# Taking the tensor work off GpSimd, and forming the low part of a weight by an adding DMA

## The chip, the cores and the metric

The program runs on one core of one Trainium2 chip, as one launch. The metric is the device time of an execution in microseconds. The kernel before took 2098.97 us (median of two runs, 2098.39 and 2099.54); its profiled execution has a span of 2094.1 us.

## The reference

Two layers of a hybrid encoder work on 512 tokens of width 1024, in float32. What matters of it:

```python
proj = h @ w_in                                   # z 1024, x/B/C 2048, dt 32, u 1024 columns
xbc  = silu(depthwise_conv_centred(xbc))          # five taps along the tokens
y    = ssd_chunked_scan(forward) + flipped(backward) + D * x      # 16 heads x 64, 4 groups, state 128
y_ssd = rms_norm(y * silu(z))
y5   = D u + Re(C s) of 64 complex diagonal recurrences, both directions   # the "S5" part
g    = gelu(y5);  y_s5 = rms_norm(g * sigmoid(g @ w_glu + b_glu))
h    = layer_norm(alpha * h + concat([y_ssd, y_s5]) @ w_out)
h    = layer_norm(alpha * h + square(relu(h @ w1)) @ w2)          # w1 1024x4096, w2 4096x1024
```

Nearly all matrix work is a product of activations with weights that are read once each: per layer 8 + 16 + 8 column tiles of w_in, 16 row blocks of w_out, 8 tiles of w_glu, 32 of w1 and 32 of w2, each 128 x 1024 floats (512 KB). Over both layers these are 240 "units".

## The kernel before, in words

**Three passes.** A product in float32 is made of three TensorE passes in the shortened type fp32r: with every operand split as high + low, `mm3` (L108 to L111) issues high x high, high x low and low x high. Each weight is split when it arrives. `load_raw` (L91) lets SP's queue bring the unit from DRAM into one of 2 buffers `raw`; `split` (L96) lets ScalarE copy it, rounded, into `whi` (L98), and then VectorE or GpSimd subtract, `wlo = raw - whi` (L99). `whi` and `wlo` have 3 buffers each. Which engine subtracts is written in a table `KN` (entries wu, wx, wz, glu); of the 224 wide units VectorE makes 166 and GpSimd 58. Sixteen units of a layer pair (the "wide" ones of `rows_proj`) are split in two halves of 512 columns.

**Stages.** Input layer norm; mixer of layer 0; its w_out in two parts (`rows_proj`, L678: the SSD half, then GLU, then the S5 half); the MLP of layer 0 (L889 up, `rows_proj` down, four quarters in turn); then the same for layer 1. In `rows_proj` four PSUM tiles rp0 to rp3 (one for each 128 tokens) take up units in pairs.

**The mixer** has two streams that a table `mrg` merges. The SSD stream (`ssd_group`, L566) works by pairs of heads: conv taps on VectorE from PSUM (L546 to L550; the last in some tiles by ScalarE and GpSimd, L554), two scans that make the decay mask E (L620, L621), the sum of two weighted copies `w + w2` (L628, GpSimd), `E * w` (L630), two products `eb` (L631, L632, GpSimd), `xd` (L592, GpSimd). The S5 stream makes input tables per batch (`s5_vtab`, L372: L385 to L387), runs a recurrence over 62 chunks (`s5_scan`, L409: four VectorE instructions of 64 elements for each of two parts at each step, L419 to L424, 992 in all), and makes output tables (`s5_wtab`, L426: L461 to L463). The tables are complex products of 512 elements, half on VectorE and half on GpSimd. Layer 0 makes its tables inside its mixer; those of layer 1 are made by a generator in between the units of layer 0's MLP, go to DRAM, and are loaded in layer 1's mixer.

**Other work of GpSimd:** squares of the MLP's hidden tiles (L904, 64 times), sums of squares for the RMS norms (L663, L665), parts of the first layer norm (L152 to L160), and powers of -0.5 for the norms (L150, L673).

**What sets the order.** Every engine runs its own instructions in one order, which a list scheduler at build time decides from priorities and a modelled time; `split` has high priority. Semaphores join the engines: a matmul of a unit waits for the split, the split for the landing of raw and for the last matmul of the unit three before.

Of the kernel before, what the change touches and what calls it, by code (L numbers as in the profile page):

```python
# [10 lines left out]
F32 = mybir.dt.float32  # L11
F32R = mybir.dt.float32r
I32 = mybir.dt.int32
AF = mybir.ActivationFunctionType
# [35 lines left out]
    wu=["GGGGGGGG", "VGGVGGGG"], wx=["GGGGGGGGGGGGGGGG", "GGGGGGGGGVGVGVGV"], wz=["GVGGGGGG", "GGGVGGGG"],  # L50
    em=["VVVVGVVG", "GGVGVVGV"], yz=["VVVVVVVG", "VVGGGVGG"], ct=["VVVVGGVVVVGVVVVV", "VVVVVVVVVGVVVVVG"], v0="VV",
    v1="GG", w0="VG", w1="GV", gv0="VG", gv1="GG", gw0="GV", gw1="VG", vb=(4, 2), gvb=(4, 3), cbb=2, wyb=4, raw=2,
    whi=3, wlo=3, nb=dict(mm=3, ss=1, sm=2, s5=2), po=[{}, {"scan": -150, "w": -35}], glu="VVVVGVVV", ln0="SVSG",
    sn=[2, 2], gen="110211101100201101103101",
# [4 lines left out]
def kernel(ctx: ExitStack, tc: tile.TileContext, A, out, depth=L):  # L59
# [80 lines left out]
    def layer_norm(pool, h, t, gb, hT, e=None):  # L140
# [10 lines left out]
        if e is G:  # L151
            G.tensor_scalar(x, x, mv[:, 0:1], rs, op0=ALU.subtract, op1=ALU.mult)  # L152
            G.tensor_tensor(x, x, gb[:, 0], op=ALU.mult)
            G.tensor_tensor(x, x, gb[:, 1], op=ALU.add)
        elif e is S:
            nb = pool.tile([128, 1], F32, tag="nb", name="nb", bufs=2)
            V.scalar_tensor_tensor(nb, mv[:, 0:1], -1.0, rs, op0=ALU.mult, op1=ALU.mult)
            S.activation(x, x, AF.Identity, scale=rs, bias=nb)
            V.tensor_tensor(x, x, gb[:, 0], op=ALU.mult)
            G.tensor_tensor(x, x, gb[:, 1], op=ALU.add)  # L160
        else:
            V.scalar_tensor_tensor(x, x, mv[:, 0:1], gb[:, 0], op0=ALU.subtract, op1=ALU.mult)
            V.scalar_tensor_tensor(x, x, rs, gb[:, 1], op0=ALU.mult, op1=ALU.add)
# [874 lines left out]
```

## Time and profile before

| | |
|---|---|
| median of the runs | 2098.97 us |
| span of the profiled execution | 2094.1 us |
| PE busy | 1754.4 us (84%) |
| DVE busy | 1418.6 us (68%) |
| POOL busy | 837.1 us (40%) |
| ACT busy | 725.5 us (35%) |
| DMA engines, mean share | q1 41.8% + q10 3.6% of 16 engines' span, 279.94 MB |

PE is TensorE, DVE VectorE, ACT ScalarE, POOL GpSimd, SP the engine that issues most loads. The busy time of an engine is a sum over stages that are bound by different things, so the rows below cut the span into stages: the start, mixer 0 and its first w_out half (0 to 633 us), GLU and second half (to 728), MLP 0 with the table generator (to 1197), mixer 1 and first half (to 1637), the rest of layer 1 (to 2065), the last norms.

### The profile page before, as it was taken

Reading aid. Unit: us, or ns where it says so; the run is one execution under the profiler, and the core shown is the slowest. Engines: PE = TensorE matmul, PEld = TensorE weight load, DVE = VectorE, ACT = ScalarE, POOL = GpSimd, SP = SyncE. Lnnn points to the kernel's source line nnn. Section 1 sums busy time; section 2 is a strip of 40 time slices with the busy share of each in tenths; the row PEclk is TensorE's granted clock in tenths of the full one; section 3 lists DMA queues with packets and bytes.
Section 4 is the critical chain, followed back from the end, with each engine's and each line's share of the span. In section 5 each row is a group of like instructions: output and inputs, shape, how many; then the busy total and the mean of one; then the engine's idle time right before and its main releaser. Section 6 shows DMA issues by size and latency. Waiting matters only on the chain.

```text
span 2094.1 us, 28322 instructions
## 1 busy us (share of the span) xinstructions
PE 1754.4 (84%) x10872; PEld 1427.8 (68%) x10872; DVE 1418.6 (68%) x2449; ACT 725.5 (35%) x1156; POOL 837.1 (40%) x557
## 2 busy tenths in 40 slices
PE   3677766676799995967899998776799999999998
PEld 3556555564578883745688887655677888888886
DVE  7468999999956767598733636999963564333335
ACT  2224433354215331211223336244563434232231
POOL 4456755445431128688702234344341112021121
PEclk8779887887799997979899999897999999999999
DMA  4655533434353355656533477542587233323232
GB/s 172 174 149 139 138 96 93 121 83 125 87 177 103 99 123 171 197 161 190 172 102 92 139 225 215 138 119 86 143 215 246 92 110 91 100 91 101 83 108 81
DMA packets 131239, 279.94 MB, mean 134 GB/s; under 512 B 12320, under 2 KB 58400, under 8 KB 130464
## 3 DMA queue, kind: packets, MB, share of 16 engines
q1 hardware_dynamic: 114144, 252.05, 41.8%
q10 hardware_dynamic: 16960, 26.09, 3.6%
q8 instruction: 85, 1.39, 0.3%
q14 instruction: 50, 0.41, 0.1%
HBM read 241.26 MB, written 36.83 MB: 133 GB/s over the span
## 4 chain that ended last, share of the span: by engine, by line
PE 44%; DVE 34%; DMA 9%; POOL 6%; issue 4%; ACT 1%; SPq 1%; POOLq 0%; DVEq 0%; ACTq 0%
PE rp L110 7%; PE rp L111 7%; PE rp L109 7%; PE up_ps L110 4%; PE up_ps L109 4%; PE up_ps L111 4%; DVE sc L422 4%; DVE XV L424 4%; DVE sc L420 4%; DVE sc L419 3%; DMA cb<-in_cb 3%; DMA Bv<-in_bb 2%; DVE E L620 2%; DVE E L621 1%; PE y L519 1%
## 5 line engine op out<-in xcount | busy, mean ns | idle before, releaser
L98 ACT ACTIVATE whi<-raw 128x1024 fp32r<-128x1024 f32 x224 | 236.2, 1057 | 494.9 <-PE rp L111 117.0
L99 DVE TENSOR_TENSOR wlo<-raw,whi 128x1024 fp32r<-128x1024 f32 x166 | 226.3, 1365 | 246.1 <-ACT whi L98 245.6
L904 POOL TENSOR_TENSOR hr<-hr 128x512 f32<-128x512 f32 x64 | 103.2, 1614 | 375.7 <-ACT hr L903 375.7
L99 POOL TENSOR_TENSOR wlo<-raw,whi 128x1024 fp32r<-128x1024 f32 x58 | 142.5, 2459 | 194.1 <-ACT whi L98 187.5
L109 PE MATMUL up_ps<-hThi,whi 128*128 128x512 f32 (+1 forms) x560 | 209.3, 376 | 3.5 <-ACT hr L903 3.2
L110 PE MATMUL up_ps<-hTlo,whi 128*128 128x512 f32 (+1 forms) x560 | 209.5, 375 | 0.1
L111 PE MATMUL up_ps<-hThi,wlo 128*128 128x512 f32 (+1 forms) x560 | 209.2, 374 | 0.0
L110 PE MATMUL rp<-wlo,ahi 128*128 128x512 f32 x448 | 184.0, 411 | 21.3 <-DVE wlo L99 21.3
L109 PE MATMUL rp<-whi,ahi 128*128 128x512 f32 x448 | 174.1, 410 | 21.5 <-ACT whi L98 13.1
L111 PE MATMUL rp<-whi,alo 128*128 128x512 f32 x448 | 182.8, 408 | 0.0
L109 PE MATMUL xbc_ps<-hThi,whi 128*128 128x512 f32 x256 | 113.6, 444 | 41.1 <-ACT z L649 23.6
L109 PEld LDWEIGHTS up_ps<-hThi,whi 128*128 128x128 f32 x560 | 105.9, 190 | 23.9 <-ACT hr L903 4.3
L111 PEld LDWEIGHTS up_ps<-hThi,wlo 128*128 128x128 f32 x560 | 106.4, 190 | 19.1 <-issue 0.4
L110 PEld LDWEIGHTS rp<-wlo,ahi 128*128 128x128 f32 x448 | 88.5, 197 | 44.8 <-DVE wlo L99 23.6
L110 PEld LDWEIGHTS up_ps<-hTlo,whi 128*128 128x128 f32 x560 | 106.3, 190 | 18.6 <-DVE hTlo L175 0.3
L109 PEld LDWEIGHTS rp<-whi,ahi 128*128 128x128 f32 x448 | 87.5, 196 | 43.8 <-ACT whi L98 14.4
L111 PE MATMUL xbc_ps<-hThi,wlo 128*128 128x512 f32 x256 | 111.2, 434 | 1.7 <-POOL wlo L99 1.7
L110 PE MATMUL xbc_ps<-hTlo,whi 128*128 128x512 f32 x256 | 111.4, 435 | 0.0
L908 DVE TENSOR_TENSOR alo<-hr,ahi 128x512 fp32r<-128x512 f32 x64 | 53.6, 839 | 76.6 <-ACT ahi L907 76.3
L111 PEld LDWEIGHTS rp<-whi,alo 128*128 128x128 f32 x448 | 88.3, 197 | 22.2
L422 DVE TENSOR_TENSOR sc<-sc,XV 128x64 f32<-128x64 f32 x248 | 101.9, 429 | 1.9
L420 DVE TENSOR_TENSOR sc<-XV,l 128x64 f32<-128x64 f32 x248 | 101.9, 411 | 0.0
(287 smaller groups left out, 4414.0 us busy)
## 6 DMA issues: line engine op xcount, KB each, us to landing
raw<-in_w SPq DMA_DIRECT2D x128, 512.0 KB
raw<-in_wi SPq DMA_DIRECT2D x64, 512.0 KB
Pv<-pd SPq DMA_DIRECT2D x32, 512.0 KB
ab<-ad SPq DMA_DIRECT2D x32, 512.0 KB
eb<-ad SPq DMA_DIRECT2D x32, 512.0 KB
raw<-in_wo SPq DMA_DIRECT2D x32, 512.0 KB
Bv<-in_bb SPq DMA_DIRECT2D x16, 512.0 KB
U<-Ud SPq DMA_DIRECT2D x128, 64.0 KB
```

The lines of the kernel that those rows point to most:

```text
L98: S.activation(hi, raw, AF.Copy)
L99: e.tensor_tensor(lo, raw, hi.bitcast(F32), op=ALU.subtract)
L109: PE.matmul(o, lhsT=sh, rhs=mh, start=first, stop=False)
L110: PE.matmul(o, lhsT=sh, rhs=ml, start=False, stop=False)
L111: PE.matmul(o, lhsT=sl, rhs=mh, start=False, stop=last)
L419: V.tensor_tensor(t2[i], x[:, ::-1, hs[i]], l8[:, 1, :, hs[i]], op=ALU.mult)
L420: V.tensor_tensor(t1[i], x[:, :, hs[i]], l8[:, 0, :, hs[i]], op=ALU.mult)
L422: V.tensor_tensor(t1[i], t1[i], x1[:, :, hs[i]], op=ALU.add)
L424: V.tensor_tensor(x1[:, :, hs[i]], t1[i], t2[i], op=ALU.add)
L620: V.tensor_tensor_scan(E2, ab[:, 0], C("md"), NEG, op0=ALU.add, op1=ALU.max)
L904: G.tensor_tensor(r, r, r, op=ALU.mult)
L908: V.tensor_tensor(hl, r, hh.bitcast(F32), op=ALU.subtract)
```

## The change

- **Weight split.** `whi` as before. `wlo` is now filled by ScalarE with the negated rounded weight (a second copy with scale -1), and then a DMA on GpSimd's queue reads the unit a second time from DRAM and adds it into `wlo` (224 DMAs of 512 KB and 32 of 256 KB). VectorE and GpSimd have no part in a split any more.
- **GpSimd's tensor work** goes to VectorE: conv tap, `w + w2`, all `E * w`, `eb`, `xd` (now read from PSUM), gate product, sums of squares, first layer norm. The square of a hidden tile is made twice: ScalarE squares into `ahi`, VectorE computes max(o,0) * r from PSUM. GpSimd keeps the -0.5 powers, a few memsets and the adding DMAs.
- **S5 tables**: for each batch and direction three VectorE products of 1024 elements in place of six of 512 on two engines. For this the sign is carried by a third slot (B, cp), and the powers lie in a replicated table `pw2`.
- **Recurrence**: one part of 128 elements in place of two of 64 (`sn` from 2 to 1): 496 instructions.
- **eb** is loaded as two pieces of 384 columns, 128 KB less for each head; buffers `vb` (4,2) to (3,2), `gvb` (4,3) to (3,2).

```diff
-    def split(hi, lo, raw, e):
+    def split(hi, lo, raw, src):
         with tc.high_priority():
             S.activation(hi, raw, AF.Copy)
-            e.tensor_tensor(lo, raw, hi.bitcast(F32), op=ALU.subtract)
+            S.activation(lo, raw, AF.Copy, scale=-1.0)
+            G.dma_start(lo, src, accum_op=ALU.add)
...
-            for ri, e in enumerate((e0, e1)[dd]):
-                t1 = pool.tile([128, 512], F32, tag="tv%d" % (e is G), name="tv", bufs=1)
-                e.tensor_tensor(v4(W[:, ri]), P[:, :, 0], v4(B[:, ri]), op=ALU.mult)
-                e.tensor_tensor(v4(t1), P[:, :, 1], v4(B[:, 1 - ri]), op=ALU.mult)
-                e.tensor_tensor(W[:, ri], W[:, ri], t1, op=ALU.add if ri else ALU.subtract)
+            t1 = pool.tile([128, 2, 512], F32, tag="tv", name="tv", bufs=1)
+            pb = lambda r: P[:, :, r].unsqueeze(1).to_broadcast([128, 2, 4, 128])
+            V.tensor_tensor(v4(W), pb(0), v4(B[:, 1:3]), op=ALU.mult)
+            V.tensor_tensor(v4(t1), pb(1), v4(B[:, 0:2]), op=ALU.mult)
+            V.tensor_tensor(W, W, t1, op=ALU.add)
...
-                G.tensor_tensor(xd, X[:, c0:c0 + 3].rearrange("p c (h q) -> p c h q", h=2),
+                V.tensor_tensor(xd, Xp[:, c0:c0 + 3].rearrange("p c (h q) -> p c h q", h=2),
...
-                G.tensor_tensor(w, w, w2, op=ALU.add)
+                V.tensor_tensor(w, w, w2, op=ALU.add)
                 Ev = E.rearrange("p (c n) -> p c n", c=4)
-                EN[KN["em"][l][ct]].tensor_tensor(Ev, Ev, w, op=ALU.mult)
-                G.tensor_tensor(eb[:, 0, 128:512], CT[:, 128:512], eb[:, 0, 128:512], op=ALU.mult)
-                G.tensor_tensor(eb[:, 1, 0:384], CT[:, 0:384], eb[:, 1, 0:384], op=ALU.mult)
+                V.tensor_tensor(Ev, Ev, w, op=ALU.mult)
+                V.tensor_tensor(eb[:, 0], CT[:, 128:512], eb[:, 0], op=ALU.mult)
+                V.tensor_tensor(eb[:, 1], CT[:, 0:384], eb[:, 1], op=ALU.mult)
...
                     S.activation(r, o, AF.Relu)
-                    G.tensor_tensor(r, r, r, op=ALU.mult)
                     hh = pool.tile([128, T], F32R, tag="ahi", name="ahi", bufs=8)
                     hl = pool.tile([128, T], F32R, tag="alo", name="alo", bufs=8)
-                    S.activation(hh, r, AF.Copy)
+                    S.activation(hh, r, AF.Square)
+                    V.scalar_tensor_tensor(r, o, 0.0, r, op0=ALU.max, op1=ALU.mult)
                     V.tensor_tensor(hl, r, hh.bitcast(F32), op=ALU.subtract)
```

GpSimd in the first mixer, before: splits, tables and SSD products stand in one queue.

```order
L99 TENSOR_TENSOR wlo<-raw,whi 128x1024 [waits DMAHW3_49,PE_49,Activation_49]
L631 TENSOR_TENSOR eb<-xbc,eb 128x384 [waits DMAHW0_49]
L632 TENSOR_TENSOR eb<-xbc,eb 128x384
L386 TENSOR_TENSOR tv<-Pv,Bv 128x512 [waits Pool_49]
...
L628 TENSOR_TENSOR w<-w,w_1781 128x512 [waits DVE_49,Activation_49]
L99 TENSOR_TENSOR wlo<-raw,whi 128x1024 [waits DMAHW3_49,PE_49,Activation_49]
L387 TENSOR_TENSOR Wv<-Wv,tv 128x512 [waits Pool_49]
L99 TENSOR_TENSOR wlo<-raw,whi 128x1024 [waits DMAHW6_49,PE_49,Activation_49]
L592 TENSOR_TENSOR xd<-Xrow,fac 128x384 [waits Activation_49]
```

The same queue after the change, from the start to the end of layer 0's first MLP units.

```order
L145 TENSOR_TENSOR rs<-ve,mhalf 128x1 x2
L94 DMA wlo<-in_wi 128x1024 x2
L145 TENSOR_TENSOR rs<-ve,mhalf 128x1 x2
L94 DMA wlo<-in_wi 128x1024 x30
L94 DMA wlo<-in_wo 128x1024 x5
L668 TENSOR_TENSOR r_ssd<-r_ssd,mhalf 128x4
L94 DMA wlo<-in_wo 128x1024 x3
L94 DMA wlo<-in_wg 128x1024 x8
...
L94 DMA alo<-in_wo 128x512 x6
L94 DMA wlo<-in_w 128x1024 x3
L145 TENSOR_TENSOR rs<-ve,mhalf 128x1 x4
L94 DMA wlo<-in_w 128x1024 x56
```

Nothing is left there but DMAs and small powers, and a power stands behind the DMAs written before it. Next, TensorE at the end of a w2 pair in the last MLP, before (names with their buffer numbers):

```order
L110 MATMUL rp2_15887<-wlo_15952,ahi_15677 128x512
L111 MATMUL rp2_15887<-whi_15951,alo_15678 128x512
L109 MATMUL rp0_15885<-whi_15957,ahi_15715 128x512 [waits Activation_49]
L109 MATMUL rp1_15886<-whi_15957,ahi_15715 128x512
L109 MATMUL rp2_15887<-whi_15957,ahi_15715 128x512
L109 MATMUL rp3_15888<-whi_15951,ahi_15639 128x512
L110 MATMUL rp3_15888<-wlo_15952,ahi_15639 128x512
L111 MATMUL rp3_15888<-whi_15951,alo_15640 128x512
L110 MATMUL rp0_15885<-wlo_15958,ahi_15715 128x512 [waits DVE_49]
```

and the place that corresponds to it after:

```order
L104 MATMUL rp0_15182<-whi_15257,ahi_15006 128x512 [waits Activation_49]
L104 MATMUL rp1_15183<-whi_15257,ahi_15006 128x512
L104 MATMUL rp2_15184<-whi_15257,ahi_15006 128x512
L105 MATMUL rp3_15185<-wlo_15251,ahi_14967 128x512
L106 MATMUL rp3_15185<-whi_15250,alo_14968 128x512
L104 MATMUL rp3_15185<-whi_15257,ahi_15006 128x512
L104 MATMUL up_ps_15325<-hThi_12735,whi_15320 128x512 [waits Activation_49]
L105 MATMUL up_ps_15325<-hTlo_12736,whi_15320 128x512
L105 MATMUL rp0_15182<-wlo_15258,ahi_15006 128x512 [waits DMASW3_49]
```

The first low-weight matmul of a unit waits for a DMA where it waited for VectorE, and more high-weight matmuls are drawn ahead of it; between the last use of the buffer's old content (wlo_15189) and this row stand 37 matmuls of 512 columns, 36 at the pair before. Last, ScalarE in such a pair after the change; before, there was one row for each unit, `whi`.

```order
L901 ACTIVATE ahi<-hr 128x512 [waits Activation_49]
L93 ACTIVATE wlo<-raw 128x1024 [waits DMAHW1_49,DMASW4_49,PE_49]
L92 ACTIVATE whi<-raw 128x1024 [waits PE_49]
L93 ACTIVATE wlo<-raw 128x1024 [waits DMAHW2_49,DMASW5_49,PE_49]
L92 ACTIVATE whi<-raw 128x1024 [waits PE_49,Activation_49]
```

The negated copy waits for raw, for the DMA that filled the buffer before, and for TensorE's last use of it; the next `whi` is queued behind it.

## Rows read from the trace of the kernel before

**Rows 1.** Windows by stage: busy us (and instructions) of each engine, clock, DMA.

```profile
core 0: us, PE busy (x) PEld busy (x) DVE busy (x) ACT busy (x) POOL busy (x), PEclk, DMA share, GB/s
0.00:633.00 633.00, 437.11 (x3387) 350.09 (x3388) 522.56 (x1010) 218.27 (x386) 330.86 (x223) 0.83 0.46 129
633.00:728.00 95.00, 95.00 (x424) 77.35 (x423) 62.49 (x76) 41.19 (x59) 17.99 (x13) 1.00 0.36 110
728.00:1197.00 469.00, 401.86 (x2193) 324.27 (x2192) 310.39 (x379) 119.02 (x169) 254.37 (x159) 0.92 0.49 147
1197.00:1637.00 440.00, 371.75 (x2840) 307.02 (x2839) 322.19 (x755) 203.12 (x358) 157.65 (x113) 0.92 0.59 171
1637.00:2065.00 428.00, 428.00 (x1947) 352.29 (x1946) 182.84 (x206) 143.89 (x188) 70.33 (x46) 1.00 0.32 97
```

**Rows 2.** Page, part 4: the chain that ended last, by engine.

```profile
PE 44%; DVE 34%; DMA 9%; POOL 6%; issue 4%; ACT 1%; SPq 1%; POOLq 0%; DVEq 0%; ACTq 0%
```

**Rows 3.** Timeline of DVE around 411 and 420 us: start, us, line.

```profile
411.33 0.25 DVE L419 TENSOR_TENSOR sc<-XV,l 128x64 f32<-128x64 f32 x1
...
417.78 1.22 DVE L621 TENSOR_TENSOR_SCAN E<-ab,E 128x512 f32<-128x512 f32 x1
...
419.87 1.00 DVE L420 TENSOR_TENSOR sc<-XV,l 128x64 f32<-128x64 f32 x1
...
421.77 2.42 DVE L420 TENSOR_TENSOR sc<-XV,l 128x64 f32<-128x64 f32 x1
```

**Rows 4.** Timeline of POOL, same stretch.

```profile
419.77 1.02 POOL L631 TENSOR_TENSOR eb<-xbc,eb 128x384 f32<-128x384 f32 x1
...
421.75 2.37 POOL L99 TENSOR_TENSOR wlo<-raw,whi 128x1024 fp32r<-128x1024 f32 x1
```

**Rows 5.** Windows of tile sc (recurrence), both mixers.

```profile
0.00:633.00 633.00, 200.76 (x496) 0.83 0.46 129
1197.00:1637.00 440.00, 162.31 (x496) 0.92 0.59 171
```

**Rows 6.** Windows of tile E on DVE (scans and products), both mixers.

```profile
0.00:633.00 633.00, 61.68 (x44) 0.83 0.46 129
1197.00:1637.00 440.00, 52.23 (x40) 0.92 0.59 171
```

**Rows 7.** Windows of tile wlo on DVE, both mixers.

```profile
0.00:633.00 633.00, 13.17 (x10) 0.83 0.46 129
...
1197.00:1637.00 440.00, 19.31 (x15) 0.92 0.59 171
```

**Rows 8.** Lines of DVE, 0 to 633 us: costliest and cheapest table line.

```profile
L461 DVE TENSOR_TENSOR Wy<-cp,pw 128x512 f32<-128x512 f32 x16 | 20.5, 1295 | 3.2 <-PE y L519 3.0
...
L463 DVE TENSOR_TENSOR Wy<-Wy,tw 128x512 f32<-128x512 f32 x16 | 15.4, 960 | 0.0
```

**Rows 9.** Lines by form, DVE, whole span: busy us, mean ns.

```profile
L645 DVE SCALAR_TENSOR_TENSOR xbc<-xbc,sp,y_ps 128x512 f32<-128x512 f32 x16 | 11.8, 740 | 6.8 <-PE y_ps L638 6.8
L99 DVE TENSOR_TENSOR alo<-raw,ahi 128x512 fp32r<-128x512 f32 x16 | 10.5, 688 | 12.0 <-ACT ahi L98 12.0
L253 DVE TENSOR_TENSOR pp_tb<-pw 128x128 f32<-128x128 f32 x4 | 1.1, 280 | 0.0
```

**Rows 10.** Tile wlo on DVE: duration in ns, min/median/max.

```profile
L99 DVE TENSOR_TENSOR wlo<-raw,whi x166: 1204/1225/2311, 182.2 to 2052.4; 128x1024 fp32r<-128x1024 f32 x166
```

**Rows 11.** Page, part 3: queue of the hardware DMAs.

```profile
q1 hardware_dynamic: 114144, 252.05, 41.8%
```

**Rows 12.** Windows: the slice of 50 us with the highest DMA share.

```profile
1550.00:1600.00 50.00, 47.96 (x465) 37.83 (x464) 17.22 (x28) 26.38 (x46) 16.03 (x15) 0.97 0.88 263
```

**Rows 13.** Timeline of SP's queue: a raw unit of 512 KB is issued.

```profile
1700.77 3.60 SPq L93 DMA_DIRECT2D raw<-in_w  x2
```

**Rows 14.** Timeline of ACT: the copy that waited for that unit.

```profile
1704.39 1.06 ACT L98 ACTIVATE whi<-raw 128x1024 fp32r<-128x1024 f32 x1 [1.84 <-DMA raw<-in_w]
```

**Rows 15.** Tile wlo on POOL: duration in ns, min/median/max.

```profile
L99 POOL TENSOR_TENSOR wlo<-raw,whi x58: 2335/2390/4258, 16.7 to 1650.1; 128x1024 fp32r<-128x1024 f32 x58
```

More of the change, by code (lines that the diff above doesn't have):

```diff
@@ L49 @@
           0, 0, 1, 1, 1, 0, 0, 0, 0, 5, 0, 0, 0, 2, 0, 0, 1, 0, 0, 0]],
[L50 to L54, printed above, removed]
+    vb=(3, 2), gvb=(3, 2), cbb=2, wyb=4, raw=2, whi=3, wlo=3, nb=dict(mm=3, ss=1, sm=2, s5=2),
+    po=[{}, {"scan": -150, "w": -35}], sn=[1, 1], gen="110211101100201101103101",
 )
@@ L128, in proj_tile, with proj_halves @@
         return o
-    def proj_halves(srcs, act, tag, name, es):
-        ws = [wunit(x, e) for x, e in zip(srcs, es)]
+    def proj_halves(srcs, act, tag, name):
+        ws = [wunit(x) for x in srcs]
         os_ = [psum(tag[i % len(tag)], name) for i in range(len(srcs))]
@@ L150, in layer_norm @@
         G.tensor_tensor(rs, ve, mhalf[:, 0:1], op=ALU.pow)
[L151 to L163, printed above, removed]
+        V.scalar_tensor_tensor(x, x, mv[:, 0:1], gb[:, 0], op0=ALU.subtract, op1=ALU.mult)
+        V.scalar_tensor_tensor(x, x, rs, gb[:, 1], op0=ALU.mult, op1=ALU.add)
         if hT is None:
@@ L256, in params @@
             V.tensor_tensor(o[:, 1], ta[:, 1, :, 0:m], tb_[:, 1, :, 0:m], op=ALU.add)
+        pw2 = per.tile([128, 2, 2, 8, 8, 8], F32, tag="pw2", name="pw2", bufs=1)
+        for ri in range(2):
+            for dd in range(2):
+                for x in range(2):
+                    S.activation(pw2[:, ri, dd, :, :, 4 * x:4 * x + 4],
+                                 pw[:, ri, dd, 1:9].rearrange("p k (m q) -> p k m q", q=4), AF.Copy)
         pd = dr.tile([2, 8, 32, 2, 128], F32, tag="pd", name="pd", bufs=2)
@@ L493, in s5_tables @@
         for m in range(8):
-            for dd, W in enumerate(s5_vtab(l, pool, prm, m, ens(KN["gv0"]), ens(KN["gv1"]), *KN["gvb"])):
+            for dd, W in enumerate(s5_vtab(l, pool, prm, m, *KN["gvb"])):
                 nc.scalar.dma_start(tb["V"][m, dd], W)
@@ L497, in s5_tables @@
         for m in range(8):
-            for dd, W in enumerate(s5_wtab(l, pool, prm, tb["KK"], m, "sm", ens(KN["gw0"]), ens(KN["gw1"]))):
+            for dd, W in enumerate(s5_wtab(l, pool, prm, tb["KK"], m, "sm")):
                 nc.scalar.dma_start(tb["W"][m, dd], W.rearrange("p r q i h -> p r (q i h)"))
@@ L615, in ssd_group @@
                 ab = pool.tile([128, 2, T], F32, tag="ab", name="ab", bufs=1)
-                eb = pool.tile([128, 2, T], F32, tag="eb", name="eb", bufs=2)
-                for i, x in enumerate((ab, eb)):
-                    nc.sync.dma_start(x,
-                                      dtp["ad"][:, hh, i].rearrange("d c s -> d (c s)").unsqueeze(0).to_broadcast([128, 2, T]))
+                eb = pool.tile([128, 2, 384], F32, tag="eb", name="eb", bufs=2)
+                nc.sync.dma_start(ab, dtp["ad"][:, hh, 0].rearrange("d c s -> d (c s)").unsqueeze(0).to_broadcast(
+                    [128, 2, T]))
+                for dd in range(2):
+                    nc.sync.dma_start(eb[:, dd], dtp["ad"][dd, hh, 1, 1 - dd:4 - dd].rearrange(
+                        "c s -> (c s)").unsqueeze(0).to_broadcast([128, 384]))
                 V.tensor_tensor_scan(E2, ab[:, 0], C("md"), NEG, op0=ALU.add, op1=ALU.max)
@@ L696, in rows_proj @@
                         lo = pool.tile([128, 512], F32R, tag=tl, name=tl, bufs=8)
-                        split(hi, lo, raw[:, i * 512:(i + 1) * 512], V)
+                        split(hi, lo, raw[:, i * 512:(i + 1) * 512], units[n, q][:, i * 512:(i + 1) * 512])
                         ws.append((hi, lo))
@@ L757 @@
         G.memset(XV[:, :, :, 0::127], 0.0)
-        os_ = proj_halves([A["wi"][l, 16 + m] for m in range(3)], act, ["mm"], "u_ps", ens(KN["wu"][l]))
+        os_ = proj_halves([A["wi"][l, 16 + m] for m in range(3)], act, ["mm"], "u_ps")
         with pool_("dt%d" % l) as pool:
@@ L769, in s5_stream @@
                     if i < 8:
-                        o = os_[i] if i < 3 else proj_tile(A["wi"][l, 16 + i], act, "mm", "u_ps", EN[KN["wu"][l][i]])
+                        o = os_[i] if i < 3 else proj_tile(A["wi"][l, 16 + i], act, "mm", "u_ps")
                         if i % 2 == 0:
@@ L897, in mlp_up @@
                 if q == 0:
-                    os_ = proj_halves([A["w1"][l, m] for m in range(3)], act, ["s5", "s5", "mm"], "up_ps", [V] * 3)
+                    os_ = proj_halves([A["w1"][l, m] for m in range(3)], act, ["s5", "s5", "mm"], "up_ps")
                 hid = []
```

90 lines of the change are left out of this document (43 added, 47 removed).

## The prediction

> **What bounds the kernel now.** I read the windows by stage first [rows 1], since the page's busy shares mix stages. In the last long one (1637 to 2065 us) TensorE is busy for all of its 428 us at full clock: it is the bound, and a unit costs 428/80 = 5.35 us there (80 units). The same holds for 633 to 728 us. In the first 633 us TensorE is busy for 437 us only and VectorE for 523; in mixer 1 (440 us) it is 372 and 322; in MLP 0 (469 us) it is 402, although MLP 1 does the same 64 units in about 64 x 5.35 = 342. So time can be won in three stages, 633 + 469 + 440 us, and none in the other 523 us. The chain of waits agrees: 44% on TensorE, 34% on VectorE, 9% on DMAs, 6% on GpSimd [rows 2].
>
> Why VectorE is that busy is seen in the timeline. A recurrence instruction of 64 elements takes 0.25 us while GpSimd is idle; at 419.87 us one takes 1.00 and at 421.77 one takes 2.42, and these are the lengths of the GpSimd instructions that run at the same moments, 1.02 and 2.37 [rows 3, 4]. Instructions of the two engines exclude each other, and the short one is charged with the long one's time. That is how 496 instructions come to 200.8 us in mixer 0 and 162.3 in mixer 1 [rows 5].
>
> **The change part by part, first VectorE.** With no GpSimd tensor work left I use undisturbed prices: 0.28 us for 128 elements and 0.69 for 512 [rows 9], 1.22 for 1024 [rows 10] and for a scan [rows 3], 0.74 for 512 from PSUM [rows 9].
>
> Mixer 0 (before: 522.6 busy, 110 idle):
> - recurrence: 200.8 becomes 248 x 0.28 = 69.4, so -131.4 [rows 5, 9].
> - splits: -13.2 [rows 7].
> - E: 61.7 becomes 32 x 1.22 + 16 x 0.69 = 49.9, so -11.8, the products moved from GpSimd counted in [rows 6].
> - tables: six lines of 16 instructions, between 20.5 and 15.4 us each, 108.9 together [rows 8]; they become 96 x 1.22 = 117, so +8.1. The 96 that GpSimd made come free, since one instruction now does two.
> - moved from GpSimd: 16 sums w at 0.69, 32 eb at 0.55 (384 elements, between the prices for 128 and 512), 16 xd at 0.6, 3 taps at 0.74, a gate product, 8 sums of squares at 0.69, about 5 us of layer norm: +51.6.
>
> The sum is 425.9 us. I keep the idle 110 us, which the diff does not touch: 536 in place of 633, **-97**. For mixer 1 the same list gives 322.2 - 92.9 - 19.3 - 2.3 + 47 = 255, with its idle 118 us 373 in place of 440: -67, if nothing else binds there. In MLP 0 VectorE has 310 us; minus 91 for splits (58 at the prices above), plus at most 117 for tables and 24 for squares from PSUM, it stays under 360 and bounds nothing.
>
> **ScalarE** gets 240 copies of 1.06 us [rows 14], 254 us: 261 of 536 in mixer 0, about 187 in MLP 0, 246 in mixer 1, 287 of 523 in the rest. It is hidden everywhere; if it were not, it would show as idle TensorE behind `whi`.
>
> **The adding DMA** is not in this trace. 240 unit loads of 512 KB come on top, and two prices are unknown: the time that it takes of the 16 DMA engines, and its delay. For the first: in the last stage a plain unit takes 0.32 x 428 / 80 = 1.71 us of all engines [rows 1]; the queue's total, 41.8% of 2094 for 252 MB, gives 1.82 [rows 11]. A plain load is one read and one write; the adding one reads DRAM, reads the buffer and writes it. The lower end is 1.71 (the second read is free), the upper 5.13 (three plain transfers). I take three movements in place of two, 1.5 x 1.71 = 2.57, because it is the nearest to the row of a plain load. Engine time then is: mixer 0, 0.46 x 633 = 291 plus 40 x 2.57; MLP 0, 0.49 x 469 = 230 plus 64 x 2.57; mixer 1, 0.59 x 440 = 260 less 7 (2 MB of eb not loaded, at 3.47 us/MB) plus 40 x 2.57; the rest, 0.36 x 95 + 0.32 x 428 = 171 plus 96 x 2.57. The engines were 88% busy in the busiest 50 us [rows 12], so I divide by 0.88: 448, 448, 405 and 475 us. Against the other bounds: mixer 0 stays at 536 by VectorE; MLP 0 goes from 469 to 448 (**-21**, no longer by GpSimd or VectorE but by the DMA engines); mixer 1 from 440 to 405 (**-35**, and not -67); the rest stays at 523 by TensorE (0).
>
> The Trainium skill speaks against this price: its page "Collectives: The Full Stack", section "The bandwidth ceiling", says that a transfer which adds needs two source reads and so runs at half the rate of a copy (32.35 against 62.28 GB/s). No run here shows it yet; by that rule the sum is that of the second rival below.
>
> **The delay.** A `wlo` buffer was refilled 1.2 us after `whi`; now a copy of 1.06 us and a landing follow its release. At the tight units, about one in each of the 40 `rows_proj` pairs, 36 matmuls stand between the release and the first use, and 50 or so elsewhere. At 5.35/24 = 0.223 us a matmul that is 8.0 us. A plain unit lands 3.6 us after its issue [rows 13, 14]; with the extra engine time it is 4.5, and I take 5 with GpSimd's issue. 1.06 + 5 + 0.4 for two hand-overs (an estimate) = 6.5: hidden, with 1.5 us to spare. At a stage's start the first low matmul has no earlier work to hide behind; I count 2 us at each of ten such places, **+20**. There the norm's power on GpSimd also stands behind DMAs that wait for buffers.
>
> **Sum:** -97 - 21 - 35 + 20 = -133. The span 2094.1 becomes 1961; with the 4.9 us by which the median (2098.97) stands above this span, **1966 us**. About 2% (42 us) is what a measurement of this kernel can tell from no change, so faster means under 2057 and slower over 2141.
>
> **The rivals.**
> - *The adding load is as cheap as a plain one* (1.71). For it: only DRAM reads may count. Against: a second operand has to come from somewhere. MLP 0 falls to 339/0.88 = 385, mixer 1 to 373 by VectorE, and late starts vanish: -97 - 84 - 67 = -248, **1851**. Chance 0.18.
> - *It costs two plain ones* (3.42), its two reads being the limit. For it: the reads of a unit are doubled. Against: the second is not from DRAM, where the plain load's time may lie. MLP 0 510 (+41), mixer 1 443 (+3), the rest 567 (+44), mixer 0 -97, starts +20: +11, **2110**, no change. This is the rule of the page named above. Chance 0.18.
> - *The other side: the DMA engines become the bound in the stages that TensorE filled.* From 3.4 us a unit on what the mixer wins is given back; at 4.0, between the second rival and the upper end, MLP 0 is +83, mixer 1 +29, the rest +108: +143, **2242**; at 5.13 it would be 2527. For it: 523 us of the kernel have nothing to win and 96 units to lose by. Against: the share there is 0.32 now, the lowest of all stages [rows 1]. Chance 0.18.
> - *The landing is late at the tight units.* If GpSimd's issue is stretched as its splits were, by up to 4.26 - 2.34 = 1.9 us [rows 15], and the landing doubles, 7.2 + 1.9 = 9.1 us, it is 2.6 us over the 6.5 that fit, at 40 units: +104, **2070**. Chance 0.08. The Trainium skill, page "SBUF — State Buffer", section "Who interferes with whom", says that GpSimd writes the descriptors of its DMAs and can be locked out by VectorE on a shared port pair; rows 3 and 4 agree for tensor instructions, and no run shows it for DMAs.
>
> The rest, 0.38, is the forecast; a price between 2.1 and 3.0 us gives it 1909 to 2020 by the same sums.
>
> **The numbers.** The range has to reach the cheap rival at 1851 and the second at 2110, and leaves out the 0.18 of the other side: 1845 to 2140. Faster: 0.38 + 0.18 and half of the late landing, 0.60; the same: 0.18 and the other half, 0.22; slower 0.18.
>
> **What the profile after would show.** Recurrence instructions near 0.28 us with a maximum not far above, some 140 us in both mixers together; VectorE near 426 and 255 us in the two mixers; GpSimd nearly empty; no idle TensorE before the low-weight matmuls of the last MLP, which still takes about 5.35 us a unit; a DMA share of about (137 + 80 x 2.57)/428 = 0.80 there. If that share is 0.64 the cheap rival holds; if it is near 0.9 with TensorE idle behind `wlo` DMAs, one of the two dear ones. If the recurrence keeps instructions of over 1 us, the exclusion was not GpSimd's doing and the whole gain in the mixers falls. If VectorE falls as said and the first stage stays near 630 us, its idle 110 us was not independent: then the S5 stream waits for `wlo` DMAs, late in a queue that GpSimd works off in order.

## The result: 1.6% slower, and the profile after

The changed kernel takes 2129.53 us (median of two runs, 2127.45 and 2131.61) against 2098.97: a ratio of 1.0159, 95% interval [1.0127, 1.0191]. The forecast was 1966 us, 6% faster; the time lies in the range, but near its far end, and on the other side of no change. The profiled execution has a span of 2125.7 us, 31.6 more than before.

The windows of the kernel after, in the columns of [rows 1], cut at the first matmul of each stage; shown are mixer 0, MLP 0, mixer 1 and MLP 1, and the two GLU stages stand in the table of the experiments:

```profile
0.00:599.70 599.70, 424.93 (x3404) 342.73 (x3404) 414.12 (x841) 260.84 (x441) 43.98 (x54) 0.86 0.68 172
...
699.10:1158.20 459.10, 403.75 (x2160) 319.83 (x2160) 220.53 (x370) 185.42 (x250) 63.77 (x72) 0.93 0.85 222
1158.20:1637.00 478.80, 383.75 (x2868) 313.67 (x2868) 260.61 (x580) 234.80 (x391) 37.44 (x43) 0.90 0.76 198
...
1737.10:2125.70 388.60, 363.56 (x1624) 296.24 (x1624) 90.41 (x133) 163.38 (x202) 62.60 (x70) 0.98 0.76 171
```

VectorE's busy time in the mixers (third engine) came out close to the forecast, 414 and 261 us. The mixers did not follow: mixer 0 is 600 us, and mixer 1 is 479, longer than before. The DMA share is 0.68 to 0.85 where it was 0.32 to 0.59 [rows 1], and GLU (both layers) and MLP 1, filled by TensorE before, have grown by 40 us together.

The chain that ended last of the kernel after, by engine, against [rows 2]:

```profile
DMA 30%; issue 28%; PE 21%; DVE 11%; ACT 5%; POOL 4%; SPq 2%; POOLq 0%; ACTq 0%; DVEq 0%
```

VectorE went from 34% to 11%, and DMAs from 9% to 30%: a part of what was VectorE's turned into waits for transfers. A part as large shows no cause: "issue", time in which the engine waited for nothing that the profile shows, went from 4% to 28%. That the exclusion of VectorE and GpSimd is gone is seen in the durations (ns, min/median/max) of a recurrence line, before and after; its longest instruction took 2399 ns and takes 414:

```profile
L419 DVE TENSOR_TENSOR sc<-XV,l x248: 229/261/2399, 188.4 to 1535.4; 128x64 f32<-128x64 f32 x124
```

```profile
L413 DVE TENSOR_TENSOR sc<-XV,l x124: 348/377/414, 254.6 to 1529.6; 128x128 f32<-128x128 f32 x124
```

The queue of the adding DMAs, which is new beside q1 of [rows 11] (packets, MB, share of 16 engines), and the row of the adding DMAs of w1 and w2 (count, KB, median us from issue to landing):

```profile
q0 software_dynamic: 36864, 125.85, 32.9%
...
wlo<-in_w POOLq DMA_DIRECT2D x120, 512.0 KB, 8.0
```

An adding unit takes 0.329 x 2125.7 / 240 = 2.91 us of the engines (I took 2.57) and lands after 8.0 us (I took 5).

### The profile page after: what moved, and what is told of

It reads as the page before. It is cut to its first block, busy times and chain, and to the rows that moved or that the text cites. A ratio compares the mean times of both kernels' runs of the same rounds, so it can differ in the third digit from the quotient of the medians.

```text
span 2125.7 us, 27962 instructions
## 1 busy us (share of the span) xinstructions
PE 1765.8 (83%) x10872; PEld 1423.7 (67%) x10872; DVE 1074.3 (51%) x2044; ACT 953.7 (45%) x1433; POOL 252.7 (12%) x287
## 4 chain that ended last, share of the span: by engine, by line
DMA 30%; issue 28%; PE 21%; DVE 11%; ACT 5%; POOL 4%; SPq 2%; POOLq 0%; ACTq 0%; DVEq 0%
DMA Bv<-in_bb 4%; DMA Ud<-us 3%; POOL wlo L94 3%; DMA cb<-in_cb 3%; PE y L516 3%; DMA wlo<-in_w 2%; DMA eb<-ad 2%; DMA U<-Ud 2%; DMA ab<-ad 2%; PE rp L105 2%; PE rp L106 2%; PE rp L104 2%; DMA Gt<-KKd 1%; PE glu_ps L104 1%; PE glu_ps L105 1%
## 5 line engine op out<-in xcount | busy, mean ns | idle before, releaser
L93 ACT ACTIVATE wlo<-raw 128x1024 fp32r<-128x1024 f32 x224 | 234.4, 1047 | 195.7 <-PE rp L105 136.3
L94 POOL DMA_DIRECT2D wlo<-in_w x120 | 103.6, 866 | 660.6 <-ACT wlo L93 623.4
L104 PE MATMUL rp<-whi,ahi 128*128 128x512 f32 x448 | 167.9, 405 | 0.1
L902 DVE SCALAR_TENSOR_TENSOR hr<-up_ps,hr 128x512 f32<-128x512 f32 x64 | 44.1, 691 | 232.6 <-ACT ahi L901 232.6
L912 DVE TENSOR_TENSOR h<-h,rp 128x512 f32<-128x512 f32 x64 | 43.6, 685 | 222.8 <-PE rp L106 222.8
L94 POOL DMA_DIRECT2D wlo<-in_wi x64 | 55.4, 866 | 598.2 <-ACT wlo L93 551.5
L104 PE MATMUL xbc_ps<-hThi,whi 128*128 128x512 f32 x256 | 108.0, 422 | 14.3 <-ACT z L644 7.3
L105 PE MATMUL xbc_ps<-hTlo,whi 128*128 128x512 f32 x256 | 106.5, 416 | 0.0
L106 PE MATMUL xbc_ps<-hThi,wlo 128*128 128x512 f32 x256 | 105.4, 412 | 1.3 <-DMA wlo<-in_wi 1.3
L379 DVE TENSOR_TENSOR Wv<-Pv,Bv 128x1024 f32<-128x1024 f32 x32 | 38.9, 1223 | 91.3 <-issue 36.9
```

Source lines behind the costliest of these rows:

```text
L93: S.activation(lo, raw, AF.Copy, scale=-1.0)
L94: G.dma_start(lo, src, accum_op=ALU.add)
L104: PE.matmul(o, lhsT=sh, rhs=mh, start=first, stop=False)
L105: PE.matmul(o, lhsT=sh, rhs=ml, start=False, stop=False)
L106: PE.matmul(o, lhsT=sl, rhs=mh, start=False, stop=last)
L379: V.tensor_tensor(v4(W), pb(0), v4(B[:, 1:3]), op=ALU.mult)
```

## The experiments

Each run was timed in three rounds beside the kernel before on the same chip; the ratio and its 95% interval are to those. Stages of the profiled executions, in us (each from the first matmul of the stage to that of the next; "mixer" includes the first half of w_out, "GLU" the second):

| run | mixer 0 | GLU 0 | MLP 0 | mixer 1 | GLU 1 | MLP 1 | span |
|---|---|---|---|---|---|---|---|
| before | 637.0 | 91.9 | 464.9 | 444.0 | 91.9 | 364.4 | 2094.1 |
| after | 599.7 | 99.4 | 459.1 | 478.8 | 100.1 | 388.6 | 2125.7 |
| e1 low part on VectorE | 620.0 | 92.6 | 412.8 | 460.7 | 92.6 | 364.9 | 2043.6 |
| e2 plain second load | 590.2 | 93.9 | 427.9 | 450.0 | 95.3 | 368.9 | 2026.2 |
| e3 before, with the add | 638.0 | 99.3 | 474.1 | 455.2 | 103.2 | 389.0 | 2158.8 |
| e4 four wlo buffers | 663.3 | 97.5 | 461.2 | 502.5 | 96.4 | 386.9 | 2207.8 |
| e5 half the decay load | 607.9 | 92.6 | 413.3 | 444.3 | 92.6 | 364.9 | 2015.6 |
| e6 = e1, two-part scan | 609.5 | 92.6 | 412.7 | 428.1 | 92.6 | 365.1 | 2000.6 |
| e7 before, MLP off GpSimd | 641.8 | 91.9 | 403.2 | 442.3 | 91.9 | 364.4 | 2035.5 |
| e8 add in mixer 0 only | 613.6 | 94.0 | 411.2 | 458.9 | 92.6 | 365.2 | 2035.5 |
| e9 after, two-part scan | 613.0 | 98.1 | 456.2 | 451.9 | 103.2 | 386.5 | 2108.9 |
| e10 add from SBUF | 612.5 | 113.2 | 504.8 | 475.0 | 114.2 | 412.9 | 2232.6 |
| e11 = e6, negation on VectorE | 594.4 | 92.6 | 417.5 | 434.5 | 92.9 | 364.9 | 1996.8 |
| e12 copy on VectorE | 631.6 | 103.0 | 475.0 | 486.8 | 100.8 | 411.6 | 2208.8 |
| e13 = after, both mended | 602.1 | 97.6 | 470.4 | 450.8 | 96.1 | 390.6 | 2107.6 |
| e14 = e11, decay rows apart | 592.3 | 92.6 | 418.9 | 418.9 | 92.9 | 365.6 | 1981.2 |

A new edit gives the scheduler a new order, so a stage moves by some us for that alone; e2 is the exception, its order is that of after on every engine. And each stage is read from one execution, while executions of one kernel lie up to 28 us apart (e13: 2105.3 to 2133.4). So a difference of 10 or 15 us in one mixer is not shown by one run alone.

### e1: the adding DMA taken out

```diff
-            S.activation(lo, raw, AF.Copy, scale=-1.0)
-            G.dma_start(lo, src, accum_op=ALU.add)
+            V.tensor_tensor(lo, raw, hi.bitcast(F32), op=ALU.subtract)
```

> The kernel after, except that the low part is again raw - whi, now always on VectorE; no adding DMA and no negated copy on ScalarE. Theory A (the adding DMA took back what VectorE won, by the time it takes of the DMA engines and by late landings): GLU and last MLP return to the 91.9 and 355.6 us of the kernel before, mixer 0 falls from 600 to about 570 (VectorE 414 + 49 of splits + 110 idle), mixer 1 from 479 to about 430, MLP 0 from 459 to 430 or less; in all about 1990 us. Theory B (the mixers were never bound by VectorE; they wait for loads and for each other, whatever the split does): the last MLP recovers, but the mixers stay near 600 and 479 and the time near 2090.

Measured: 2039.55 us, ratio 0.974 [0.972, 0.976]. GLU and MLP 1 are back at 92.6 and 364.9, MLP 0 is at 413: there theory A holds in full. In the mixers neither holds: mixer 0 rose to 620 (it has 40 splits more on VectorE) and VectorE is idle for 161 us of it, mixer 1 fell to 461 and is still 17 above before. Without the DMA the rest of the change gains 2.6%, two fifths of what was forecast for the whole.

### e2: the same transfers, without the addition

```diff
-            G.dma_start(lo, src, accum_op=ALU.add)
+            G.dma_start(lo, src)
```

> The kernel after with the second load of a unit as a plain copy in place of an adding one (what stands in wlo is then the weight itself, not its low part). Same instructions, same order, same bytes from DRAM. If the sum costs (a second read inside the chip), a unit takes about 1.75 us of the engines in place of 2.91 (699 us of queue time over 240 units), lands 1 to 2 us sooner than 8.0, and the time falls by 30 to 70 us. If the second transfer as such costs, whatever it does, the time stays within 10 us of 2130.

Measured: 2028.43 us, ratio 0.970 [0.967, 0.973]; span 99.5 us under after, more than the 30 to 70 expected, 31 of it in MLP 0, 29 in mixer 1, 20 in MLP 1. Queue and landing of this run:

```profile
q0 software_dynamic: 36864, 125.85, 19.6%
...
wlo<-in_w POOLq DMA_DIRECT2D x120, 512.0 KB, 4.7
```

A plain second load takes 0.196 x 2026.2 / 240 = 1.65 us of the engines, the adding one 2.91 with the same bytes from DRAM: the adding load is 1.76 times a copy, and lands 3 us later. In GLU and the MLPs it is mostly the addition that costs the time: after stands 84 us above e1 there, which has no second load; of these the addition is 61 (after against e2), and the plain second load with its copies on ScalarE 23 (e2 against e1). In mixer 0 it is not: there e2 is only 9 us under after.

### e3: the adding DMA alone, in the kernel before

```diff
-            e.tensor_tensor(lo, raw, hi.bitcast(F32), op=ALU.subtract)
+            S.activation(lo, raw, AF.Copy, scale=-1.0)
+            G.dma_start(lo, src, accum_op=ALU.add)
```

> The kernel before with the split of the kernel after alone (negated copy on ScalarE, adding DMA on GpSimd's queue); all tensor work of GpSimd stays there. Theory A: about +40 us in GLU and last MLP, as after, and more in the mixers, where GpSimd issues each DMA behind its tensor work: 2150 to 2250 us. If it is close to 2100 or below, the adding DMA is not what cost the time, and the moves to VectorE are.

Measured: 2157.07 us, ratio 1.029 [1.025, 1.033], as theory A said. GLU and MLP 1 are those of after (99, 103, 389), +43 us together. In mixer 0, where it takes 49 us of busy time off VectorE, nothing is won (638).

### e4: a fourth wlo buffer

```diff
-    vb=(3, 2), gvb=(3, 2), cbb=2, wyb=4, raw=2, whi=3, wlo=3, nb=dict(mm=3, ss=1, sm=2, s5=2),
+    vb=(3, 2), gvb=(3, 2), cbb=2, wyb=3, raw=2, whi=3, wlo=4, nb=dict(mm=3, ss=1, sm=2, s5=2),
```

> The kernel after with 4 wlo buffers in place of 3 (and 3 buffers Wy in place of 4, to make room). The matmuls between a buffer's release and its next use rise from 36 to 50 or more at the tight places. If the landing's delay (8.0 us) against the time to hide it is what idles TensorE in the MLPs, the waits for wlo there (19.7 + 6.9 us in MLP 0, 12.6 + 1.9 in MLP 1) go to nearly 0 and the time falls by 30 to 45 us. If the DMA engines' time is the bound, the waits move to raw or whi and the time falls by less than 15.

Measured: 2207.01 us, ratio 1.054 [1.051, 1.057]. The mixers are not read, since Wy (the output tables of S5) lost a buffer there. In MLP 1, which has no Wy, the time is 386.9 against 388.6. Waits in that stage (total us, times, longest), of the kernel after on TensorE and ScalarE:

```profile
PE rp L105 <- DMA wlo<-in_w: 12.6, 9, 3.4
...
ACT wlo L93 <- DMA raw<-in_w: 28.0, 5, 6.1
```

and of e4 on ScalarE, where TensorE no longer waits for wlo of w2:

```profile
ACT wlo L93 <- DMA raw<-in_w: 96.6, 23, 6.8
```

The wait only moved, from the adding DMA behind TensorE to the raw load behind ScalarE, with evictions queued after it. So the landing is late at the tight places, as the fourth rival said, but room for it buys nothing while the loads themselves come late.

### e5: half of the decay load

```diff
-                ab = pool.tile([128, 2, T], F32, tag="ab", name="ab", bufs=1)
+                ab = pool.tile([128, T], F32, tag="ab", name="ab", bufs=2)
```

> The run with the low part on VectorE, in which the decay rows `ab` of a head are loaded for one direction only, into 2 buffers of half the size (both scans read the forward row; the other direction's decays are left out). Theory C (with GpSimd's exclusion gone the mixers wait for loads into tiles of one buffer, ab above all: 32 us of the chain of waits in mixer 0, 47 in mixer 1): mixer 0 falls from 620 by 15 to 30 us, mixer 1 from 461 by 30 to 45, the rest stays; 1970 to 2000 us. If the wait is only handed on to the next late thing, both stay within 10 us.

Measured: 2019.56 us, ratio 0.965 [0.962, 0.969]. Mixer 0 -12, mixer 1 -16 from e1, the rest unchanged: theory C is right in kind, but both falls are smaller than it said. Part of the wait is handed on.

### e6: the recurrence in two parts again

```diff
-    po=[{}, {"scan": -150, "w": -35}], sn=[1, 1], gen="110211101100201101103101",
+    po=[{}, {"scan": -150, "w": -35}], sn=[2, 2], gen="110211101100201101103101",
```

> The run with the low part on VectorE, with the recurrence in two parts of 64 elements as before. A rival to theory C for mixer 1, which stood 17 us above the kernel before: one part of 128 makes every instruction wait for the one before it (0.38 us each in place of 0.28). If so, mixer 1 falls by 10 us or more. By theory C nothing changes beyond 5 us in either mixer.

Measured: 2002.80 us, ratio 0.957 [0.954, 0.960]. The rival to theory C was right in its number: mixer 1 falls by 33 us and mixer 0 by 10, although VectorE has more work, as the windows of mixer 1 show (e1, then e6):

```profile
1125.40:1586.10 460.70, 384.99 (x2870) 316.22 (x2869) 304.98 (x620) 196.04 (x349) 2.93 (x3) 0.90 0.56 160
```

```profile
1114.80:1542.90 428.10, 373.68 (x2869) 308.09 (x2868) 319.00 (x868) 199.16 (x351) 2.83 (x3) 0.94 0.59 172
```

319 us of VectorE against 305 and still 33 us sooner. The rival's reason, instructions that wait for the one before them, is not what the trace shows: from its first to its last instruction the recurrence of mixer 1 takes 262 us in e1 and 284 in e6, and VectorE is idle before its instructions for under 3 us in either. What differs is when it begins, and when its results can be used. Rows of tile XV (the recurrence's input and state) in mixer 1; the two times before the semicolon are the first and the last start, in us from the start of the execution. First e1, whose stage begins at 1125.4: the matmuls of the S5 outputs, a recurrence line, and the copies that fill XV:

```profile
L515 PE MATMUL y<-Wy,XV x512: 269/269/473, 1506.9 to 1582.8; 64*64 64x128 f32 x171
...
L412 DVE TENSOR_TENSOR sc<-XV,l x62: 340/374/397, 1241.3 to 1502.2; 128x128 f32<-128x128 f32 x62
...
L399 ACT ACTIVATE XV<-v_ps x16: 569/584/598, 1172.3 to 1235.3; 128x504 f32<-128x504 f32 x16
```

then e6, whose stage begins at 1114.8 and whose last copy starts at 1220.0:

```profile
L515 PE MATMUL y<-Wy,XV x512: 268/269/473, 1460.6 to 1539.6; 64*64 64x128 f32 x171
...
L412 DVE TENSOR_TENSOR sc<-XV,l x124: 233/264/290, 1196.6 to 1479.5; 128x64 f32<-128x64 f32 x124
```

A part of 64 elements needs only the first four of the eight batches in XV. So in e6 the recurrence begins 82 us into the stage, before the last copies; in e1 it begins at 116 us, after all of them. At the other end the outputs of the first four batches need only the first part: in e6 they start before the recurrence has ended, 346 us into the stage, and in e1 after its end, at 382. That is 36 us of difference, and the stage ends 33 us sooner. (The order of other instructions changed too, so the whole 33 us are not proved to be this.)

### e7: the kernel before, with its MLPs off GpSimd

```diff
-    v1="GG", w0="VG", w1="GV", gv0="VG", gv1="GG", gw0="GV", gw1="VG", vb=(4, 2), gvb=(4, 3), cbb=2, wyb=4, raw=2,
+    v1="GG", w0="VG", w1="GV", gv0="VV", gv1="VV", gw0="VV", gw1="VV", vb=(4, 2), gvb=(4, 3), cbb=2, wyb=4, raw=2,
-                    G.tensor_tensor(r, r, r, op=ALU.mult)
+                    V.tensor_tensor(r, r, r, op=ALU.mult)
```

> The kernel before with GpSimd's work in the MLPs alone on VectorE: the generated tables of layer 1 (unmerged, products of 512) and the squares of hidden tiles. Splits as before. By the exclusion of the two engines MLP 0 falls from 465 to between 410 and 430 us, as in the run with the low part on VectorE (413), though VectorE has all the work; everything else within 5 us: about 2050. If merged tables were what MLP 0 gained by, it stays over 445.

Measured: 2038.34 us, ratio 0.973 [0.971, 0.975]. MLP 0 falls from 464.9 to 403.2, more than with merged tables; the rest stays within 5 us. Its window:

```profile
733.70:1136.90 403.20, 386.46 (x2161) 307.09 (x2160) 296.35 (x523) 117.33 (x166) 10.60 (x6) 0.98 0.54 170
```

VectorE has all the work of the stage, and is busy for 296 us, less than the 310 of before, when GpSimd had a part of it [rows 1] (306 when the stage is cut at the same place). It makes 152 instructions more (523 for 371), some 105 us at 0.69 us each by [rows 9] (an estimate), and is still busy for less. That is the exclusion. The 62 us of the stage also hold that GpSimd's own products and squares were slower than VectorE's; this run does not tell the two apart.

### e8: the adding DMA in mixer 0 only

The flag is taken back after layer 0's first w_out half.

```diff
+            if ADD[0]:
                 S.activation(lo, raw, AF.Copy, scale=-1.0)
                 G.dma_start(lo, src, accum_op=ALU.add)
+            else:
+                V.tensor_tensor(lo, raw, hi.bitcast(F32), op=ALU.subtract)
```

> Adding DMA in layer 0's mixer and first w_out half only (40 units), the low part on VectorE everywhere else. From the stages of the two runs: mixer 0 as after, 600, the rest as with the low part on VectorE (92.6 + 412.8 + 460.7 + 92.6 + 364.9): 2023 of span, about 2020 us, 3.5% under the kernel before. If mixer 0's 20 us were an accident of the order, it stays near 2040.

Measured: 2033.87 us, ratio 0.971 [0.968, 0.974]. Mixer 0 took 613.6, between the two expectations. It doesn't settle what the 20 us between after and e1 are: for its first 480 us VectorE's order is that of after, and already there the same instruction stands 6 us later than in after. So a good part of the difference comes from one execution to the next, and what the adding DMA is worth to that stage is not shown.

### e9: the kernel after, with a two-part recurrence

The edit is that of e6.

> The kernel after, adding DMA and all, with the recurrence in two parts again. Without the adding DMA two parts gained 10.5 us in mixer 0 and 33 in mixer 1. If the two causes add up, the time is about 2085 (as the kernel before); if late loads hide the recurrence in the kernel after, it stays over 2110.

Measured: 2116.54 us, ratio 1.011 [1.007, 1.015], which overlaps with after. Mixer 1 fell by 27 us, mixer 0 rose by 13: the two parts pay in mixer 1 beside the adding DMA too, and do not in mixer 0.

### e10: adding from the buffer on the chip

```diff
-            G.dma_start(lo, src, accum_op=ALU.add)
+            G.dma_start(lo, raw, accum_op=ALU.add)
```

> The kernel after, with the adding DMA reading the unit from its raw buffer instead of from DRAM (so raw is held until it has landed). Theory D1 (the adding DMA is dear by the second trip to DRAM): a unit takes clearly less than 2.91 us of the engines. Theory D2 (it is dear by adding, whatever the source; the plain second load took 1.65): 2.5 us or more. The total is 2100 to 2180, since raw has 2 buffers and is now free later.

Measured: 2236.82 us, ratio 1.070 [1.063, 1.077]; slower than expected, which may be because raw is held (not tested). Its queue and its issues:

```profile
q0 software_dynamic: 36864, 125.85, 30.3%
...
wlo<-raw POOLq DMA_DIRECT2D x224, 512.0 KB, 5.4
```

0.303 x 2232.6 / 240 = 2.82 us a unit: D2. It lands sooner, but holds the engines nearly as long as with a source in DRAM.

### e11: ScalarE freed of the wait for B

```diff
-        S.activation(B[:, 0], B[:, 2], AF.Copy, scale=-1.0)
+        V.tensor_scalar(B[:, 0], B[:, 2], -1.0, None, op0=ALU.mult)
```

> The best run so far (low part on VectorE, recurrence in two parts), with the negated third slot of the B table made by VectorE in place of ScalarE, whose queue stood still for 66 us in mixer 0 and 30 in MLP 0 at that instruction, waiting for the load of B. If what is queued behind it matters, mixer 0 falls by 8 to 25 us and MLP 0 by 2 to 8: 1970 to 1992 us. If not, 2003 within 5.

Measured: 1996.93 us, ratio 0.954 [0.949, 0.960], not to be told from e6 as a whole; the 1970 to 1992 us expected were missed. Mixer 0 fell by 15, as expected, but that is within what executions differ by; MLP 0 and mixer 1 rose by 5 and 6.

### e12: the negated copy on VectorE

```diff
-            S.activation(lo, raw, AF.Copy, scale=-1.0)
+            V.tensor_scalar(lo, hi.bitcast(F32), -1.0, None, op0=ALU.mult)
```

> The kernel after, with the negated copy of 240 units on VectorE in place of ScalarE; the adding DMA stays. If ScalarE's in-order queue is a good part of the loss (it waits at that copy for a buffer, with evictions of PSUM behind it), GLU and MLPs regain over 15 us together and the time falls below 2110. If the adding DMA alone is, those stages stay within 5 us of after: 99, 459, 100, 389.

Measured: 2210.78 us, ratio 1.055 [1.050, 1.060]. Neither expectation: GLU and MLPs lose 43 us more than after. The copy now reads `whi`, so it stands in a chain of buffer release, `whi`, copy, DMA; that this chain is what costs the 43 us is argued, not shown. ScalarE's load is not shown to be harmless by this run, since two things changed.

### e13: the kernel after, with both mixer faults mended

The edits of e6 and e11 in the kernel after.

> The kernel after, adding DMA and all, with the recurrence in two parts and the negated slot of B on VectorE: the run with 594 us in mixer 0, but with the adding DMA in place of splits on VectorE. If ScalarE's wait for B and the one-part recurrence were what left VectorE idle for 186 us in mixer 0, it falls to 550 to 575 (VectorE needs 49 us less than in that run). If the second load itself keeps VectorE idle, by late loads and the copies on ScalarE, it stays at 590 or more. GLU and MLPs as after; total 2060 to 2110.

Measured: 2117.91 us, ratio 1.011 [1.005, 1.017]; the expected total of 2060 to 2110 was missed. Mixer 0 stays at 602 with VectorE busy for 422: idle 180, as in after (186), where e11 has 594 - 467 = 127. The windows of mixer 0 in e1, e11 and e13, in the columns of [rows 1]:

```profile
0.00:620.00 620.00, 433.62 (x3404) 354.60 (x3404) 458.63 (x884) 224.69 (x400) 6.79 (x11) 0.83 0.48 130
```

```profile
0.00:594.40 594.40, 430.96 (x3405) 350.04 (x3405) 467.14 (x1141) 220.91 (x392) 6.75 (x11) 0.86 0.48 135
```

```profile
0.00:602.10 602.10, 430.74 (x3404) 350.34 (x3404) 421.76 (x1097) 257.54 (x433) 43.34 (x54) 0.85 0.67 171
```

VectorE's waits for the load of B in mixer 0, in e11 and then in e13:

```profile
DVE Bv L369 <- DMA Bv<-in_bb: 28.7, 6, 11.4
```

```profile
DVE Bv L370 <- DMA Bv<-in_bb: 59.0, 8, 13.4
```

The same load, in the same code, keeps VectorE waiting twice as long beside the adding DMAs, and all its waits for loads in the stage add up to 114 us where e11 has 70. So with the two faults mended it is the second load that keeps VectorE idle, and it gives back what it takes off that engine. It is not the only thing that can: e1 has the two faults and no second load, and is idle for 620 - 459 = 161 us. Either is enough to keep most of the idle time, so in mixer 0 the causes do not add up.

### e14: decay rows in two tiles

```diff
-                ab = pool.tile([128, 2, T], F32, tag="ab", name="ab", bufs=1)
+                ab = [pool.tile([128, T], F32, tag="ab%d" % dd, name="ab%d" % dd, bufs=1) for dd in range(2)]
```

> The best run (low part and negated slot on VectorE, recurrence in two parts), with the decay rows of the two directions in two tiles, each loaded when its own scan has let it go; nothing is left out. By theory C (wait for ab, one buffer) the mixers fall by 3 to 15 us together, to 1980 to 1995; loading half of it had given 12 and 16. If the order or SP's 32 more issues count for more, 1997 or above.

Measured: 1984.99 us, ratio 0.948 [0.945, 0.950], 5.2% under the kernel before and in the range expected: the fastest version by its median, though its interval meets that of e11. Mixer 1 fell by 16 us, mixer 0 by 2.

## Why the prediction was wrong, step by step

- **Exclusion of VectorE and GpSimd: right.** The long recurrence instructions are gone, VectorE's busy time in the mixers was forecast at 426 and 255 and came to 414 and 261, and e7 shows that VectorE is busy for less with more work. That the sums came so close is in part luck: the recurrence took VectorE 89 us in mixer 0 where the sum had 69.4, and other instructions, which the sum left as they were, lost stalls too. In MLP 0 the move off GpSimd is worth 52 to 62 us (e1, e7); in the kernel after the adding DMAs left 6.
- **"I keep the idle 110 us, which the diff does not touch": the step that failed.** It became 186 us in mixer 0 and 218 (for 118) in mixer 1, where even the bound by the DMA engines that the sum took, 405 us, left room for 150 only. The mixers are 60 + 70 us of the 165 by which the span missed; MLP 0 missed by 15, and GLU and MLP 1 by 40 where the sum had 20 for stage starts. In mixer 0 two causes overlap: without the adding DMA 161 us stay idle (e1), with the recurrence in two parts and the negation of B on VectorE, but with the adding DMA, 180 (e13), and without either cause 127 (e11). In mixer 1 the 51 us from after to e6 (478.8 to 428.1) are 27 for the recurrence in one part (after against e9) and 24 for the adding DMA (e9 against e6, 451.9 and 428.1); the other 19 of the 70 stay open. With both causes gone the step holds: e11 has 127 us idle in mixer 0 and 115 in mixer 1. The prediction had named the sign, VectorE as said but the first stage near 630 us; it came half way, and VectorE's own waits there are for the loads of the mixer's tables (B, cb, ab) rather than for `wlo`.
- **"The rest stays at 523 by TensorE (0)": wrong too.** In GLU and MLP 1 a plain second load costs 8 us over e1, and the addition 30 more (e2, after).
- **The recurrence at 0.28 us an instruction: mis-sized.** It is 0.38 for 128 elements. And the count was not what mattered: in one part the recurrence begins later and hands its results on later, which in mixer 1 cost more than the saved instructions gained (e1 against e6).
- **The adding DMA at 1.5 times a plain load: mis-sized.** It is 1.76 times (e2), 2.91 us, between my forecast and the second rival. The time came out near that rival's 2110, though by another sum: 2.91 alone, put into my sum, gives mixer 0 -97, MLP 0 (230 + 64 x 2.91)/0.88 = 473 (+4), mixer 1 420 (-20), the rest 0 and starts +20, so about 2006. That the time lies near the rival's is luck. The share in MLP 1 was forecast at 0.80 and was 0.76, yet the stage lost 24 us: here the engines were not full, and loads still came late.
- **The page's rule.** The Trainium skill ("Collectives: The Full Stack", section "The bandwidth ceiling") gives, for a ring of four ranks, 62.28 / 32.35 = 1.93 between a copy and an adding transfer. The trace has 1.76 for one core's DMA: nearer to it than my three movements in place of two, 1.5. By e10 the price hardly depends on where the source lies.
- **The delay: wrong in size, the fourth rival in part right.** A landing of 8.0 us is over the 6.5 that fit, and TensorE waits at the tight places (e4). It is not GpSimd's issue that is stretched, as that rival had it; durations (ns) of the issues in the kernel after:

```profile
L94 POOL DMA_DIRECT2D wlo<-in_w x120: 862/862/1214, 676.6 to 2077.3; - x120
```

  The Trainium skill ("SBUF — State Buffer", section "Who interferes with whom") warns of GpSimd being kept from writing descriptors by VectorE; with a median equal to the minimum these 120 rows show little of that, and none of 1.9 us.
- **ScalarE hidden: right for its busy time, wrong for its order.** Its new instruction on B waits for a load with other work queued behind. Moving it went with 15 us less in mixer 0 (e11), a size that one execution does not show, and with nothing beside the adding DMA (e13).

What is left open: how much of the loss in GLU and the MLPs is ScalarE's in-order queue, which e12 did not isolate; the 19 us of mixer 1; and the 28% of the chain that the profile calls issue.

## What to carry to other kernels

When one engine's stalls are taken away, its idle time is not a constant to add back: list the loads with one buffer and the chains that come next, and price them with the new traffic on. Two causes of waiting can hide each other, so take them out one by one and together. A transfer that adds should be measured before it is used; here it costs 1.76 copies and 3 us of delay, while a subtraction on an engine with time to spare costs under 1 us in each stage (e1, GLU and MLP 1). Before two independent chains are joined to halve their instructions, look at what each waits for and who waits for it: joined, the first must wait for the inputs of the second, and its readers for the end of both.

## What the runs showed of the hardware

- An adding DMA of 512 KB takes 2.91 us of the 16 engines from DRAM and 2.82 from SBUF, a plain one on the same queue 1.65 (e10, e2). In these kernels they land after 8.0, 5.4 and 4.7 us (medians; 8.0 and 4.7 are those of w1 and w2).
- GpSimd is held for 0.86 us to issue an adding DMA (at most 1.21 in the 120 of w1 and w2), and for 0.53 to issue a plain one (e2).
- An instruction of 128x128 elements of the recurrence takes 0.37 to 0.38 us, one of the parameter products 0.28 [rows 9]; why was not tried. In mixer 1 the 248 of 128 elements keep VectorE busy for 88 us (e1), and 496 of 64 elements for 105 (e6).
- With the adding DMAs beside it, VectorE waited 59.0 us in place of 28.7 for the same loads of B (e13, e11), at a DMA share of 0.67 in place of 0.48.
